# Transposing the residual on VectorE in 32x32 blocks in place of TensorE's transposes and ScalarE's copies

## The chip, the cores and the metric

The kernel runs on one core of one Trainium2 chip. The metric is the device time of one execution in microseconds (us). Three runs of the kernel before took 1252.45, 1252.47 and 1254.14 us, median 1252.47. The engines are named as in the profile: PE is TensorE's matmuls, PEld its weight loads, DVE is VectorE, ACT is ScalarE, POOL is GpSimd, SP is SyncE, which issues most transfers.

## The reference

One decoder layer over 272 tokens (16 meta tokens and 256 of the sequence), 2048 channels, all in float32:

```
h    = concat(meta, x)                                # 272 x 2048
u    = rmsnorm(h, norm_mix)
mix  = head groups of (u @ w_in)                      # 8 retention, 4 mLSTM heads
h    = h + mix @ w_out
u    = rmsnorm(h, norm_ffn)
up   = causal_dwconv(u @ w_up) + bias                 # 3 taps, 2 x 5632 channels
h    = h + (silu(gate) * val) @ w_down
out  = rmsnorm(h, norm_final)[16:]                    # the 256 tokens of the sequence
```

The residual h of the line before the last, 256 tokens by 2048 channels, is what this document follows: the kernel holds it channel-major and needs it token-major for the last addition.

## The kernel before, in words

Activations are kept channel-major: a tile has 128 channels on the partitions and the tokens along the free dimension, and 16 such slices make up the 2048 channels. `hT` (128 x 16 x 272) is the residual in this form. Every weight is split into two parts that TensorE multiplies: `load_w` (L123) brings 512 KB into `wraw` (4 buffers), ScalarE copies it to `whi` (L129, 5 buffers), and VectorE subtracts to get `wlo` (L131, 5 buffers). A "weight tile" below is one such piece. `mmk` (L134) spends 24 matmuls on a weight tile of 8 slices: 16 with `whi` (L138 and L139, on the high and the low part of the activations), then 8 with `wlo` (L141).

The stages are: input projections and attention heads, output projection, then the FFN in two halves of 22 channel blocks each. The output projection adds its result to `hT` slice by slice (`out_tile`, L508) and makes from it the scaled `uh` (ScalarE, L509) and `ul` (VectorE, L510), and the squares, which GpSimd sums into `ssq` (L517). `norm2` (L533) turns `ssq` into the normalisation row `rstd2`: a matmul (L535), ScalarE's L164 to L167, VectorE's L168, L169 and L537.

In the FFN, channel block j has two projections (gate, s = 0, and value, s = 1) of two weight tiles each. A projection is accumulated in one PSUM tile `mmps`, of which there are 4. VectorE empties it (`cu`, L559) by a multiplication with `rstd2`; the convolution, the gate and the split into `mh` and `ml` follow on ScalarE and VectorE. After the 22 blocks of a half, `mh` and `ml` are multiplied with `w_down` into 4 column blocks of 512 in token-major form, and `done` (L620) adds each to `hn`.

`hn` (128 tokens x 2 x 2048) is the residual token-major. `transposed_h` (L548) fills it, called once, at j = 1 of the first half: 32 TensorE transposes of 128x128 blocks of `hT` against `ident`, four of them into one PSUM tile `atps`, and 8 copies by ScalarE (L555). `hn` is first read by `done`, at the end of the first half.

The program is not run in the order in which it is written. The Tile framework sorts the instructions by its own timeline estimate into one fixed order for each engine when the kernel is built, so an instruction without dependences can land far ahead of its place in the code. Each engine then executes its own list strictly in that order, and an instruction that waits holds up all behind it.

Of the kernel before, what the change touches and what calls it, by code (L numbers as in the profile page):

```python
# [10 lines left out]
F32 = mybir.dt.float32  # L11
# [5 lines left out]
P = 128  # L17
# [5 lines left out]
T0 = NMETA - 2  # L23
# [60 lines left out]
def trunk(ctx: ExitStack, tc: tile.TileContext, io, out: bass.AP):  # L84
    nc = tc.nc

    def pool(name, bufs, **kw):
        return tc.tile_pool(name=name, bufs=bufs, **kw)
# [4 lines left out]
    at = ctx.enter_context(pool("at", 4, space=PSUM))  # L93
# [4 lines left out]
    hT = hpool.tile([P, KT, T], F32, name="hT")  # L98
# [6 lines left out]
    ident = consts.tile([P, P], F32, name="ident")  # L105
# [17 lines left out]
    def load_w(src, shape, to=None):  # L123
        nonlocal last_load
        raw = wpool.tile(shape, F32, name="wraw", bufs=4)
        last_load = nc.sync.dma_start(raw, src)
        to, n = (wpool, 5) if to in (None, wpool) else (to, None)
        hi = to.tile(shape, F32R, name="whi", bufs=n)
        nc.scalar.copy(hi, raw)  # L129
        lo = to.tile(shape, F32R, name="wlo", bufs=n)  # L130
        nc.vector.tensor_tensor(out=lo, in0=raw, in1=hi.bitcast(F32), op=ALU.subtract)  # L131
        return hi, lo
# [15 lines left out]
    def project(src, xh, xl, t0):  # L148

        ps = mm.tile([P, 512], F32, name="mmps")  # L150
        for half in range(2):
            half_tile(ps[:, : xh.shape[2] - t0], src, half, xh, xl, t0)
        return ps

    def table(name, after):

        with tc.issue_after(after.ins):
            return nc.scalar.preload_act_table_set(name)
# [38 lines left out]
    with pool("sq", 1, side="right") as sqp:  # L197
        for k0, k1 in [(0, 1), (1, 2)] + [(k, k + 2) for k in range(2, KT, 2)]:
# [16 lines left out]
            for k in range(k0, k1):  # L215
                i = k - k0
# [30 lines left out]
    a = _COLS["retn"][0]  # L247
    nc.vector.tensor_scalar(out=norms[:, :RH], in0=par[:, a : a + RH], scalar1=-0.5, scalar2=None, op0=ALU.mult)

    a = _COLS["mln"][0]  # L250
# [245 lines left out]
    hn = hnp.tile([P, 2, DM], F32, name="hn")  # L496
# [36 lines left out]
    def norm2():  # L533
        ms2 = at.tile([P, 512], F32, name="atps")
        nc.tensor.matmul(ms2[:, :NQ], inv_dm, ssq, start=True, stop=True)  # L535
        r = rsqrt_m2(wk2, ms2[:, :NQ], NQ, squared)
        nc.vector.tensor_scalar(out=rstd2, in0=r[:, :NQ], scalar1=-0.5, scalar2=None, op0=ALU.mult)  # L537
# [7 lines left out]
    ss4 = midp.tile([P, 2, 4], F32, name="ss4")  # L545
    junk = midp.tile([P, 512], F32, name="junk")

    def transposed_h():  # L548
        for tt in range(2):
            for q in range(4):  # L550
                ps = at.tile([P, 512], F32, name="atps")
                for j in range(4):
                    c = T0 + 2 + tt * P
                    nc.tensor.transpose(ps[:, j * P : (j + 1) * P], hT[:, 4 * q + j, c : c + P], ident)  # L554
                nc.scalar.copy(hn[:, tt, q * 512 : (q + 1) * 512], ps)  # L555

    def conv3(ps, f, name):
        u = wk2.tile([P, NQ], F32, name="cu")
        nc.vector.tensor_tensor(out=u, in0=ps[:, :NQ], in1=rstd2, op=ALU.mult)  # L559
        o = wk2.tile([P, SEQ], F32, name=name)  # L560
        nc.scalar.activation(o, u[:, 2:], AF.Identity, scale=pcol("fw", 3 * f + 2), bias=pcol("fb", f))
        for j in range(2):
            nc.vector.scalar_tensor_tensor(out=o, in0=u[:, j : j + SEQ], scalar=pcol("fw", 3 * f + j), in1=o, op0=ALU.mult, op1=ALU.add)
        return o
# [6 lines left out]
    def finish(tt):  # L571
        v, r, t = ss[:, tt : tt + 1], r0[:, tt : tt + 1], rt[:, tt : tt + 1]
        nc.vector.reduce_sum(v, ss4[:, tt, :], axis=mybir.AxisListType.X)
        nc.scalar.activation(r, v, AF.Ln, scale=1.0 / DM, bias=epsc)
        nc.scalar.activation(r, r, AF.Exp, scale=-0.5)
        nc.vector.tensor_scalar(out=v, in0=v, scalar1=-0.5 / DM, scalar2=-0.5 * EPS, op0=ALU.mult, op1=ALU.add)
        nc.vector.scalar_tensor_tensor(out=t, in0=v, scalar=r, in1=r, op0=ALU.mult, op1=ALU.mult)
        nc.vector.scalar_tensor_tensor(out=t, in0=t, scalar=1.5, in1=r, op0=ALU.add, op1=ALU.mult)
        for q in range(4):
            h = hn[:, tt, q * 512 : (q + 1) * 512]  # L580
            if q % 2 == 0:
                nc.vector.tensor_scalar(out=h, in0=h, scalar1=t, scalar2=None, op0=ALU.mult)
            else:
                nc.scalar.activation(h, h, AF.Copy, scale=t)
            nc.sync.dma_start(out[tt * P : (tt + 1) * P, q * 512 : (q + 1) * 512], h)

    NQD = NHF // 2
    for half in range(2):
        mh = midp.tile([P, NHF, SEQ], F32R, name="mh")
        ml = midp.tile([P, NHF, SEQ], F32R, name="ml")  # L590
        for jj in range(NHF):
            j = half * NHF + jj
            pair = []
            for s in range(2):
                pair.append(project(io["wu"][2 * j + s], uh, ul, 0))
                if j == 0 and s == 0:
                    norm2()
            gt = conv3(pair[0], j, "gt")
            vt = conv3(pair[1], NF + j, "vt")
            nc.scalar.activation(gt, gt, AF.Silu)  # L600
            nc.vector.tensor_tensor(out=gt, in0=gt, in1=vt, op=ALU.mult)
            copied = nc.scalar.copy(mh[:, jj, :], gt)
            nc.vector.tensor_tensor(out=ml[:, jj, :], in0=gt, in1=mh[:, jj, :].bitcast(F32), op=ALU.subtract)
            if j == 1:
                transposed_h()
        if half == 1:
            table("natural_log_exp_and_others", copied)

        def product(ps, tt, q, w):
            hi, lo = w  # L610
            rows = slice(tt * P, (tt + 1) * P)
            for i in range(2):
                k = 2 * q + i
                nc.tensor.matmul(ps, mh[:, k, rows], hi[:, i, :], start=k == 0, stop=False)  # L614
                nc.tensor.matmul(ps, ml[:, k, rows], hi[:, i, :], start=False, stop=False)  # L615
            for i in range(2):
                k = 2 * q + i
                nc.tensor.matmul(ps, mh[:, k, rows], lo[:, i, :], start=False, stop=k == NHF - 1)  # L618

        def done(ps, tt, b):  # L620
            h = hn[:, tt, b * 512 : (b + 1) * 512]
            nc.vector.tensor_tensor(out=h, in0=ps, in1=h, op=ALU.add)
            if half == 1:
                nc.scalar.activation(junk, h, AF.Square, accum_out=ss4[:, tt, b : b + 1])
                nc.gpsimd.tensor_tensor(out=h, in0=h, in1=gfin[:, b * 512 : (b + 1) * 512], op=ALU.mult)

        if half == 1:
            wk2_cm.__exit__(None, None, None)
            up_cm.__exit__(None, None, None)
            more_cm = pool("more", 4, side="right")  # L630
            more = more_cm.__enter__()
        for b in range(4):
            pss = [at.tile([P, 512], F32, name="atps") for _ in range(2)]
            last = half == 1 and b == 3

            lag = 4 if last else 0
            ws = {}
            for q in range(NQD + lag):
                if q < NQD:
                    ws[q] = load_w(io["wd"][b, half * NQD + q], [P, 2, 512], more if last and q % 2 else wpool)  # L640
                    product(pss[0], 0, q, ws[q])
                    if q == NQD - 1:
                        done(pss[0], 0, b)
                        if last:
                            finish(0)
                if q >= lag:
                    product(pss[1], 1, q - lag, ws.pop(q - lag))
            done(pss[1], 1, b)
# [84 lines left out]
```

## Time and profile before

| | us |
|---|---|
| median of three runs | 1252.47 |
| profiled execution | 1253.9 |
| its span, first to last instruction | 1252.1 |
| PE busy | 1237.2 (99%) |
| PEld busy | 1178.8 (94%) |
| DVE busy | 810.9 (65%) |
| ACT busy | 657.8 (53%) |
| mean granted TensorE clock | 0.997 |

The profiled execution is 1.4 us above the median, and 1.8 us of its time lie outside the span. The span was taken on the same program as the three runs. The busy shares are means over all stages. Times in the trace are counted from the start of the span; the output projection's last weight tile ends at 484.0 us, and the FFN begins there.

### The profile page before, as it was taken

Reading aid. Unit: us, or ns where it says so; the run is one execution under the profiler, and the core shown is the slowest. Engines: PE = TensorE matmul, PEld = TensorE weight load, DVE = VectorE, ACT = ScalarE, POOL = GpSimd, SP = SyncE. Lnnn points to the kernel's source line nnn. Section 1 sums busy time; section 2 is a strip of 40 time slices with the busy share of each in tenths; the row PEclk is TensorE's granted clock in tenths of the full one; section 3 lists DMA queues with packets and bytes.
Section 4 is the critical chain, followed back from the end, with each engine's and each line's share of the span. In section 5 each row is a group of like instructions: output and inputs, shape, how many; then the busy total and the mean of one; then the engine's idle time right before and its main releaser. Section 6 shows DMA issues by size and latency. Waiting matters only on the chain.

```text
span 1252.1 us, 22222 instructions
## 1 busy us (share of the span) xinstructions
PE 1237.2 (99%) x9094; PEld 1178.8 (94%) x9094; DVE 810.9 (65%) x1188; ACT 657.8 (53%) x885; POOL 64.1 (5%) x68
## 2 busy tenths in 40 slices
PE   8999999999999999999999999999999999999996
PEld 7999999999999999999999998888999999998885
DVE  7857677766666767667677664445776767664452
ACT  8646655655556546655555553334555555554441
POOL 0100001111110111000000000000000000000010
PEclk9999999999999999999999999999999999999999
DMA  8754554555554667555555656665655555666661
GB/s 269 228 183 136 159 156 154 174 170 173 159 166 155 178 185 218 156 185 183 185 186 179 185 177 189 192 188 185 185 183 184 175 185 184 186 181 185 189 202 68
DMA packets 63591, 224.11 MB, mean 179 GB/s; under 512 B 7388, under 2 KB 8284, under 8 KB 63360
## 3 DMA queue, kind: packets, MB, share of 16 engines
q1 hardware_dynamic: 62832, 219.92, 56.4%
q0 software_dynamic: 656, 2.76, 0.8%
q8 instruction: 71, 1.16, 0.4%
q14 instruction: 32, 0.26, 0.1%
HBM read 220.56 MB, written 2.10 MB: 178 GB/s over the span
## 4 chain that ended last, share of the span: by engine, by line
PE 98%; DVE 1%; DMA 0%; ACT 0%; issue 0%; SPq 0%; ACTq 0%; DVEq 0%
PE mmps L138 25%; PE mmps L141 25%; PE mmps L139 25%; PE atps L615 7%; PE atps L618 7%; PE atps L614 7%; PE atps L330 1%; DMA wraw<-in_w 0%; PE atps L322 0%; PE atps L307 0%; PE atps L332 0%; PE atps L331 0%; PE atps L554 0%; PE atps L323 0%; DVE xl L207 0%
## 5 line engine op out<-in xcount | busy, mean ns | idle before, releaser
L129 ACT CAST whi<-wraw 128x1024 fp32r<-128x1024 f32 x404 | 423.4, 1049 | 489.2 <-PE mmps L139 256.1
L131 DVE TENSOR_TENSOR wlo<-wraw,whi 128x1024 fp32r<-128x1024 f32 x404 | 494.9, 1226 | 200.8 <-ACT whi L129 193.6
L139 PE MATMUL mmps<-ul,whi 128*128 128x258 f32 x1408 | 345.8, 283 | 0.0
L138 PE MATMUL mmps<-uh,whi 128*128 128x258 f32 x1408 | 345.8, 282 | 0.0
L138 PEld LDWEIGHTS mmps<-uh,whi 128*128 128x128 f32 x1408 | 266.1, 189 | 0.1
L139 PEld LDWEIGHTS mmps<-ul,whi 128*128 128x128 f32 x1408 | 265.2, 188 | 0.1
L138 PE MATMUL mmps<-xh,whi 128*128 128x272 f32 (+2 forms) x880 | 224.5, 289 | 0.0
L139 PE MATMUL mmps<-xl,whi 128*128 128x272 f32 (+2 forms) x880 | 222.1, 285 | 0.0
L141 PE MATMUL mmps<-uh,wlo 128*128 128x258 f32 x1408 | 199.2, 284 | 0.0
L141 PEld LDWEIGHTS mmps<-uh,wlo 128*128 128x128 f32 x1408 | 182.4, 189 | 0.0
L138 PEld LDWEIGHTS mmps<-xh,whi 128*128 128x128 f32 x880 | 165.7, 188 | 1.3
L139 PEld LDWEIGHTS mmps<-xl,whi 128*128 128x128 f32 x880 | 165.9, 189 | 0.1
L615 PE MATMUL atps<-whi,ml 128*128 128x512 f32 x352 | 140.0, 398 | 0.0
L614 PE MATMUL atps<-whi,mh 128*128 128x512 f32 x352 | 138.0, 392 | 0.0
L141 PE MATMUL mmps<-xh,wlo 128*128 128x272 f32 (+2 forms) x880 | 129.1, 285 | 0.0
L141 PEld LDWEIGHTS mmps<-xh,wlo 128*128 128x128 f32 x880 | 116.9, 188 | 0.0
L559 DVE TENSOR_TENSOR cu<-mmps,rstd 128x258 f32<-128x258 f32 x88 | 37.6, 427 | 116.0 <-PE mmps L141 115.9
L618 PE MATMUL atps<-wlo,mh 128*128 128x512 f32 x352 | 110.4, 395 | 0.0
L615 PEld LDWEIGHTS atps<-whi,ml 128*128 128x128 f32 x352 | 66.1, 188 | 17.0
L618 PEld LDWEIGHTS atps<-wlo,mh 128*128 128x128 f32 x352 | 66.1, 188 | 16.0
L614 PEld LDWEIGHTS atps<-whi,mh 128*128 128x128 f32 x352 | 66.1, 188 | 14.9
L139 PE MATMUL mmps<-mixl,whi 128*128 128x258 f32 x256 | 63.3, 283 | 0.0
(203 smaller groups left out, 1021.5 us busy)
## 6 DMA issues: line engine op xcount, KB each, us to landing
wraw<-in_wu SPq DMA_DIRECT2D x176, 512.0 KB, 3.5
wraw<-in_wi SPq DMA_DIRECT2D x108, 512.0 KB, 3.6
wraw<-in_wd SPq DMA_DIRECT2D x88, 512.0 KB, 3.5
wraw<-in_wo SPq DMA_DIRECT2D x32, 512.0 KB, 3.6
wraw<-in_w SPq DMA_DIRECT2D x7, 320.0 KB, 5.8
out<-hn SPq DMA_DIRECT2D x8, 256.0 KB, 3.0
hT<-in_xT SPq DMA_DIRECT2D x7, 272.0 KB, 6.4
e<-in_decay POOLq DMA_DIRECT2D x8, 209.0 KB, 3.4
```

What stands on the lines that cost most here:

```text
L129: nc.scalar.copy(hi, raw)
L131: nc.vector.tensor_tensor(out=lo, in0=raw, in1=hi.bitcast(F32), op=ALU.subtract)
L138: nc.tensor.matmul(ps, hi[:, k, :], xh(kk), start=kk == first, stop=False)
L139: nc.tensor.matmul(ps, hi[:, k, :], xl(kk), start=False, stop=False)
L141: nc.tensor.matmul(ps, lo[:, k, :], xh(kk), start=False, stop=kk == last)
L330: nc.tensor.matmul(ps[:, 0:NQ], lhs(0, P), pT[:, 0:CA], start=True, stop=False)
L559: nc.vector.tensor_tensor(out=u, in0=ps[:, :NQ], in1=rstd2, op=ALU.mult)
L614: nc.tensor.matmul(ps, mh[:, k, rows], hi[:, i, :], start=k == 0, stop=False)
L615: nc.tensor.matmul(ps, ml[:, k, rows], hi[:, i, :], start=False, stop=False)
L618: nc.tensor.matmul(ps, mh[:, k, rows], lo[:, i, :], start=False, stop=k == NHF - 1)
```

## The change

`transposed_h` no longer uses TensorE, PSUM or ScalarE. It takes an index i from 0 to 3, the block of 32 channels within each slice of 128. For each of the 4 blocks a of 32 tokens and each of the 2 token tiles t, one VectorE instruction takes 32 partitions by 16 slices by 32 tokens of `hT` and writes the sixteen 32x32 blocks, each transposed, to 32 partitions of `hn`. That is 8 instructions for one i and 32 in all, each with 512 elements per partition on 32 partitions. In the code the calls are spread over j = 1 to 4.

```diff
-    def transposed_h():
-        for tt in range(2):
-            for q in range(4):
-                ps = at.tile([P, 512], F32, name="atps")
-                for j in range(4):
-                    c = T0 + 2 + tt * P
-                    nc.tensor.transpose(ps[:, j * P : (j + 1) * P], hT[:, 4 * q + j, c : c + P], ident)
-                nc.scalar.copy(hn[:, tt, q * 512 : (q + 1) * 512], ps)
+    def transposed_h(i):
+
+        src = hT[32 * i : 32 * (i + 1), :, T0 + 2 :].rearrange("p k (t a e) -> p k t a e", t=2, e=32)
+        for a in range(P // 32):
+            dst = hn[32 * a : 32 * (a + 1), :, :].rearrange("p t (k f) -> p k t f", f=P)
+            for t in range(2):
+                nc.vector.transpose(dst[:, :, t, 32 * i : 32 * (i + 1)], src[:, :, t, a, :])
...
-            if j == 1:
-                transposed_h()
+            if 1 <= j <= 4:
+                transposed_h(j - 1)
```

The built programs show where the instructions land. On VectorE, at the change from the output projection to the FFN, the list before reads as follows; the first row is the addition to the last slice of `hT`, `ul` is the last low part of the activations, L168 to L537 make `rstd2`, and L559 empties the first FFN projection:

```order
L508 TENSOR_TENSOR hT<-mmps,hT 128x258
L131 TENSOR_TENSOR wlo<-wraw,whi 128x1024
L510 SCALAR_TENSOR_TENSOR ul<-hT,par,uh 128x258
L131 TENSOR_TENSOR wlo<-wraw,whi 128x1024 x2
L168 SCALAR_TENSOR_TENSOR rt<-atps,rt 128x258
L169 SCALAR_TENSOR_TENSOR r_5863<-rt,r_5863 128x258
L537 TENSOR_SCALAR rstd_84<-r_5863 128x258
L559 TENSOR_TENSOR cu<-mmps,rstd_84 128x258
```

Between the last `hT` and the first `cu` stand 3 weight tiles' `wlo` (one row of one and one row of two) and four small operations. The list of the changed kernel has at the same place, first part:

```order
L508 TENSOR_TENSOR hT<-mmps,hT 128x258
L131 TENSOR_TENSOR wlo<-wraw,whi 128x1024
L554 STREAM_TRANSPOSE hn<-hT 32x16x32 x9
L510 SCALAR_TENSOR_TENSOR ul<-hT,par,uh 128x258
L554 STREAM_TRANSPOSE hn<-hT 32x16x32 x6
L131 TENSOR_TENSOR wlo<-wraw,whi 128x1024
L554 STREAM_TRANSPOSE hn<-hT 32x16x32 x3
L168 SCALAR_TENSOR_TENSOR rt<-atps,rt 128x258
L554 STREAM_TRANSPOSE hn<-hT 32x16x32 x2
L131 TENSOR_TENSOR wlo<-wraw,whi 128x1024
L554 STREAM_TRANSPOSE hn<-hT 32x16x32 x4
```

All calls have moved ahead of the place where they stand in the code: 24 of the 32 transposes stand in these rows, behind the last `hT` and among the steps that make `rstd2`. The rest follows on VectorE, with the tiles' own numbers (`wlo_6246` is the low part of the thirteenth weight tile of the FFN; `cu_5933` empties the first projection, `mmps_5800`):

```order
L131 TENSOR_TENSOR wlo_6045<-wraw_6041,whi_6043 128x1024 [waits DMAHW4_49,PE_49,Activation_49]
L131 TENSOR_TENSOR wlo_6100<-wraw_6096,whi_6098 128x1024 [waits DMAHW5_49,PE_49,Activation_49]
L554 STREAM_TRANSPOSE hn_4707<-hT_70 32x16x32 x4
L169 SCALAR_TENSOR_TENSOR r0_5863<-rt_5867,r0_5863 128x258 [waits DVE_49]
L554 STREAM_TRANSPOSE hn_4707<-hT_70 32x16x32
L131 TENSOR_TENSOR wlo_6130<-wraw_6126,whi_6128 128x1024 [waits DMAHW6_49,PE_49,Activation_49]
L554 STREAM_TRANSPOSE hn_4707<-hT_70 32x16x32 x3
L131 TENSOR_TENSOR wlo_6161<-wraw_6157,whi_6159 128x1024 [waits DMAHW7_49,PE_49,Activation_49]
L131 TENSOR_TENSOR wlo_6191<-wraw_6187,whi_6189 128x1024 [waits DMAHW0_49,PE_49,Activation_49]
L537 TENSOR_SCALAR rstd2_84<-r0_5863 128x258 [waits DVE_49]
L131 TENSOR_TENSOR wlo_6246<-wraw_6242,whi_6244 128x1024 [waits DMAHW1_49,PE_49,Activation_49]
L558 TENSOR_TENSOR cu_5933<-mmps_5800,rstd2_84 128x258 [waits DVE_49]
```

The first `cu` now stands behind all 32 transposes and behind eight `wlo` that follow the first transpose (one and one in the fence above, and six here). On TensorE the 32 transposes are gone, and at the start of the fifth projection, `mmps_6095`, which is the next user of the PSUM buffer of `mmps_5800`, the list reads:

```order
L141 MATMUL mmps_6010<-uh_4711,wlo_6045 128x258 [waits DVE_49]
L141 MATMUL mmps_6010<-uh_4711,wlo_6045 128x258 x7
L138 MATMUL mmps_6095<-uh_4711,whi_6098 128x258 [waits DVE_49,Activation_49]
L139 MATMUL mmps_6095<-ul_4712,whi_6098 128x258
```

Before, 16 of the transposes stood between the two projections here; now the fifth projection follows directly, with a wait for VectorE.

## The prediction

> **What bounds the kernel now.** I read the page's busy table and the chain that ended last first.
>
> ```profile
> span 1252.1 us, 22222 instructions
> PE 1237.2 (99%) x9094; PEld 1178.8 (94%) x9094; DVE 810.9 (65%) x1188; ACT 657.8 (53%) x885; POOL 64.1 (5%) x68
> PE 98%; DVE 1%; DMA 0%; ACT 0%; issue 0%; SPq 0%; ACTq 0%; DVEq 0%
> L131 DVE TENSOR_TENSOR wlo<-wraw,whi 128x1024 fp32r<-128x1024 f32 x404 | 494.9, 1226 | 200.8 <-ACT whi L129 193.6
> ```
>
> TensorE is the bound: it is busy nearly throughout and carries 98% of the chain. So a matmul removed is time saved, and a microsecond in which TensorE stands still is a microsecond lost, since nothing later has slack to give it back. VectorE's 65% is a mean; what matters is how far it may fall behind at the place of the change. Next came the transposes themselves and the timeline around them.
>
> ```profile
> L554 PE MATMUL atps<-ident,hT x32: 270/273/273, 507.6 to 513.3; 128*128 128x128 f32 x32
> 507.61 1.91 PE L554 MATMUL atps<-ident,hT 128*128 128x128 f32 x16
> 509.27 0.37 PE L138 MATMUL mmps<-uh,whi 128*128 128x258 f32 x1
> 502.03 0.43 DVE L559 TENSOR_TENSOR cu<-mmps,rstd 128x258 f32<-128x258 f32 x1 [0.50 <-PE mmps L141]
> 507.81 0.43 DVE L559 TENSOR_TENSOR cu<-mmps,rstd 128x258 f32<-128x258 f32 x1 [1.55 <-PE mmps L141]
> 517.09 0.43 DVE L559 TENSOR_TENSOR cu<-mmps,rstd 128x258 f32<-128x258 f32 x1 [1.61 <-PE mmps L141]
> 522.87 0.43 DVE L559 TENSOR_TENSOR cu<-mmps,rstd 128x258 f32<-128x258 f32 x1 [1.51 <-PE mmps L141]
> ```
>
> A `cu` starts when TensorE has finished a projection. These follow one another by 5.78 us (502.03 to 507.81, and 517.09 to 522.87); across the transposes it is 9.28 us.
>
> **What is removed.** 9.28 − 5.78 = 3.5 us of TensorE; the first 16 transposes, 507.61 to 509.27, give 1.66, which doubled is 3.3. I take **−3.5 us**, and it is on the bounding engine. ScalarE's eight copies go too, worth nothing: ScalarE waits for buffers that TensorE frees (its 53%).
>
> **What is added: 32 VectorE instructions of unknown price.** The trace has no transpose on VectorE. Each has 512 elements per partition. The rows nearest to it:
>
> ```profile
> L213 DVE TENSOR_TENSOR wlo<-wraw,whi 128x512 fp32r<-128x512 f32 x7 | 4.8, 686 | 1.1 <-ACT whi L211 1.1
> L559 DVE TENSOR_TENSOR cu<-mmps,rstd 128x258 f32<-128x258 f32 x88 | 37.6, 427 | 116.0 <-PE mmps L141 115.9
> L582 DVE TENSOR_SCALAR hn<-hn,frt 128x512 f32<-128x512 f32 x4 | 1.8, 484 | 0.1
> L537 DVE TENSOR_SCALAR rstd<-r 128x258 f32<-128x258 f32 x1 | 0.3, 297 | 0.0
> L262 DVE TENSOR_TENSOR kT<-kT,rstd 4x272 f32<-4x272 f32 x1 | 0.4, 430 | 0.0
> 493.55 1.22 DVE L131 TENSOR_TENSOR wlo<-wraw,whi 128x1024 fp32r<-128x1024 f32 x1
> 494.68 1.00 DVE L563 SCALAR_TENSOR_TENSOR gt<-cu,par,gt 128x256 f32<-128x256 f32 x2
> ```
>
> L559 to L131 (427 ns for 258, 1226 ns for 1024 elements) is 1.04 ns per element and 158 ns fixed. L262 shows that 4 partitions cost what 128 do, so using 32 partitions at a time saves nothing: the transposes cost four times what whole-width ones would. At one element per step each takes 0.69 us (the 512-element row, 686 ns). Independent neighbours can overlap by 0.08 us or so (493.55 + 1.22 − 494.68 = 0.09), so the low side of this case is 0.61; one block's 32 further steps for filling would give 0.72. Single-source operations in SBUF run about twice as fast (L537, 297 ns); for 512 elements that is 158 + 267 = 0.43, less overlap 0.35, the **lower bound**. Two steps per element, as a 1024-element operation, give 1.23 us, the **upper bound**. I take 0.69: a transpose moves single elements between partitions, and that row has its size.
>
> The Trainium skill, "VectorE: DVE Perf Modes", section "The three transpose paths", gives 311 ns for a 128x128 bf16 transpose on VectorE, in 32x32 blocks only; at its 0.96 GHz a further 384 elements make 0.71 us, an estimate, by which the sum below would be 0.7 us higher. Its rules for kernel authors give a 128x128 transpose to TensorE if PSUM will do, which speaks against the change. No run here shows either yet.
>
> **Where they lie.** All 32 have been sorted ahead of the first `cu`, into the start of the FFN, where VectorE must also deliver `wlo` and `rstd2`. I replay VectorE's list from rows:
>
> ```profile
> 484.03 0.28 PE L138 MATMUL mmps<-uh,whi 128*128 128x258 f32 x1
> 484.57 1.22 DVE L131 TENSOR_TENSOR wlo<-wraw,whi 128x1024 fp32r<-128x1024 f32 x1
> 485.70 0.98 DVE L510 SCALAR_TENSOR_TENSOR ul<-hT,par,uh 128x258 fp32r<-128x258 f32 x1
> 485.67 0.74 POOL L517 TENSOR_TENSOR ssq<-ssq,s2b 128x258 f32<-128x258 f32 x1 [0.63 <-ACT s2b L516]
> 491.95 0.43 DVE L168 SCALAR_TENSOR_TENSOR rt<-atps,rt 128x258 f32<-128x258 f32 x1 [0.56 <-ACT rt L167]
> 492.41 0.43 DVE L169 SCALAR_TENSOR_TENSOR r<-rt,r 128x258 f32<-128x258 f32 x1
> 493.20 0.43 DVE L559 TENSOR_TENSOR cu<-mmps,rstd 128x258 f32<-128x258 f32 x1
> 506.88 1.05 ACT L129 CAST whi<-wraw 128x1024 fp32r<-128x1024 f32 x1 [1.57 <-issue]
> wraw<-in_wu SPq DMA_DIRECT2D x176, 512.0 KB, 3.5
> ```
>
> The first transpose starts at 484.57 + 1.22 = 485.8, when the last `hT` is written. From there to the end of the first `cu` VectorE has: 32 transposes of d us; eight `wlo`, 9.6 (1.2 each: 1.22, starting up to 0.09 early); L168, L169, L537 and `cu`, 0.43 + 0.43 + 0.30 + 0.43 = 1.6; and the last `ul`, 0.5. (L510 takes 0.98 here beside GpSimd's addition, 485.67, and half that elsewhere; the first transposes will now meet this addition in its place, which evens out.) The sum is 11.7 + 32 d, so `cu` ends at **497.5 + 32 d**: at 0.69, 519.6.
>
> TensorE meanwhile: the first eight FFN weight tiles (numbered from 0) run from 484.03 to 507.61, where the transposes started before. They fill all four `mmps`, and the fifth projection needs the buffer that the first `cu` frees. What else they need comes in time or just late. The last `ul` would come at 485.8 + 9 d + 0.5 = 492.5, but was moved behind in TensorE's list too, to some 494.5 by its pace of 2.89 us a tile (half of 5.78). The `wlo` of tiles 5, 6 and 7 come at about 497.8, 502.9 and 506.9; TensorE asks for them at about 500.7, 503.6 and 506.6. So TensorE is held for 0.3 us there and then stands until `cu`: together 519.6 − 507.6 = **12.0 us**, against none before. VectorE, in turn, waits for nothing in this stretch: the `wraw` behind a `wlo` comes some 3.5 us after its buffer is free, and `whi` another 1.05 later (506.88).
>
> Afterwards, `whi` and `wlo` of tiles 8 to 12 are ready when TensorE resumes, 14 us of work; the two delayed channel blocks' gates and convolutions, some 8 us on VectorE and ScalarE by the same rows, are done before tile 13's `wlo` is asked for. So no second gap follows, and none of the first is recovered.
>
> **The clock.** A pause of TensorE costs more than itself, as the start of this trace shows:
>
> ```profile
> 19.69 0.28 PE L139 MATMUL mmps<-xl,whi 128*128 128x262 f32 x1
> 21.22 0.39 PE L141 MATMUL atps<-xh,wlo 128*128 128x272 f32 x1 [1.25 <-DVE wlo L213]
> 21.60 0.43 PE L138 MATMUL atps<-xh,whi 128*128 128x272 f32 x1
> 24.95 0.28 PE L141 MATMUL mmps<-xh,wlo 128*128 128x262 f32 x1
> 25.07 0.29 PE L138 MATMUL atps<-xh,whi 128*128 128x272 f32 x1
> 23.00:24.00 1.00, 1.00 (x6) 1.00 (x6) 1.00 (x1) 0.99 (x2) 0.00 (x0) 0.50 0.97 377
> ```
>
> After a gap of 1.25 us in an already sparse stretch the granted clock was 0.50, and from 21.60 to 24.95 the 15 matmuls came 0.22 us apart in place of 0.12: 15 × 0.10 = **1.5 us** more. A gap of 12 us should bring the same once; a price of nothing is the other bound.
>
> The Trainium skill, "TensorE: Matmul & The Clock Gate", section "HAM oscillation — how this bites in real kernels", puts the drop at gaps over about 3.4 us; by that rule too a 12 us gap pays it, and this trace shows the drop after less.
>
> **The sum.** −3.5 + 12.0 + 1.5 = **+10.0 us**. On the profiled execution (span 1252.1, in all 1253.9) that is a span of 1262.1 and 1263.9 in all; the median of the runs lies 1.4 below the profiled one, so I forecast 1252.5 + 10.0 = **1262.5 us**. With d from 0.61 to 0.73 and the clock price from 0 to 1.5, this case runs from +5.9 (9.4 − 3.5) to +11.3: 1258 to 1264. Break-even is a gap of 2.0 us (2.0 + 1.5 = 3.5), `cu` at 509.6, so d = 0.38.
>
> **Rivals.**
>
> *Transposes at twice the rate* (0.35 us). For it: they have one source, in SBUF, as L537 has. Against: L537 does not cross partitions. `cu` would be ready at 508.7 but for its neighbour in the list, `wlo` of tile 12, whose `whi` waits for TensorE to finish tile 7's L139; 506.88 + 1.05, then 1.22 and 0.43 put `cu` at 509.7. The gap is 2.1, the sum −1.4 to +0.1: about 1251.5, **not slower**. At 0.43 `cu` ends at 511.3: +0.2 to +1.7.
>
> *The gap doesn't arise.* If VectorE's list caught up by its idle third, only −3.5 would be left: **1249.0**. The page's 65% speaks for it; the fixed list against it, since the first `cu` cannot pass the transposes.
>
> *Half the rate* (1.23 us). `cu` ends at 536.9, the gap is 29.3, the sum +27.3: **1279.8**. For it: 32-bit elements, rows of only 32, and a filling of the block that may not overlap the emptying. Against: no row with two steps per element except special operations.
>
> **How the numbers follow.** My case 0.70, twice the rate 0.10, no gap 0.05, slower transposes 0.15. A difference under 0.2% (2.5 us) can't be told from none here. Slower comes from my case and the slow one, 0.85; the fast one is mostly no difference, 0.10; faster needs the gap away, 0.05. The likeliest case alone has 1258 to 1264. The range takes in the fast rates, and on the slow side prices up to about 1.05 us (1274): 1252 to 1274 leaves out the missing gap and most of the slow case, under 2 in 10. The two bounds of d give 1251 and 1280.
>
> **What would show it.** L554 as a VectorE group of 32 with a mean near 0.69 us; starts between 485.8 and 517; a TensorE gap of about 12 us ending when the first `cu` ends, near 519.6, on `mmps`; the granted clock at 0.50 for some 3 us behind it; no further gap; TensorE's steps across j = 1 at 5.78. The forecast is wrong if the mean is under 0.4 us or far over 0.75, if the first `cu` starts near 493 as before, or if TensorE runs on past tile 7.

## The result

| | before | changed |
|---|---|---|
| median, us | 1253.76 (5 runs, 1252.45 to 1254.46) | 1262.63 (5 runs, 1261.79 to 1262.83) |
| ratio | | 1.0076, 95% interval 1.0065 to 1.0087 |
| profiled execution, span in us | 1252.1 | 1260.9 |

The changed kernel is slower by 0.76%, 9.5 us by the interval's centre (8.9 between the two medians). Forecast were 1262.5 us and 10.0 us more than before.

Its page shows a TensorE that is idle at one place. These are the span, the 40 slices of TensorE's busy share and of its clock, and two groups of part 5 (busy us, mean ns of one, then the idle time ahead of them and what ended it):

```profile
span 1260.9 us, 22186 instructions
PE   8999999999999999699999999999999999999996
PEclk9999999999999999799999999999999999999999
L138 PE MATMUL mmps<-uh,whi 128*128 128x258 f32 x1408 | 346.6, 283 | 11.2 <-DVE cu L558 11.2
L131 DVE TENSOR_TENSOR wlo<-wraw,whi 128x1024 fp32r<-128x1024 f32 x404 | 494.7, 1226 | 197.4 <-ACT whi L129 192.7
```

In the seventeenth slice, which begins at 504 us, TensorE falls to 6 tenths and its clock to 7. L138 waited 11.2 us for a `cu`; before, the same group waited for nothing:

```profile
L138 PE MATMUL mmps<-uh,whi 128*128 128x258 f32 x1408 | 345.8, 282 | 0.0
```

(Line numbers behind the edit are smaller by one in the changed kernel: `cu` is L558.) The price of a transpose, in the group by shape, is

```profile
L554 DVE STREAM_TRANSPOSE hn<-hT 32x512 f32<-32x512 f32 x32 | 21.1, 685 | 0.4
```

685 ns each, 21.1 us in all. VectorE's timeline from the last `hT` to the first `cu` (start, duration, then the operation and how many in a row) is the replay of the prediction with its real numbers:

```profile
482.91 0.43 DVE L508 TENSOR_TENSOR hT<-mmps,hT 128x258 f32<-128x258 f32 x1 [0.44 <-PE mmps L141]
483.26 1.22 DVE L131 TENSOR_TENSOR wlo<-wraw,whi 128x1024 fp32r<-128x1024 f32 x1
484.39 5.93 DVE L554 STREAM_TRANSPOSE hn<-hT 32x512 f32<-32x512 f32 x9
490.35 0.49 DVE L510 SCALAR_TENSOR_TENSOR ul<-hT,par,uh 128x258 fp32r<-128x258 f32 x1
490.87 4.04 DVE L554 STREAM_TRANSPOSE hn<-hT 32x512 f32<-32x512 f32 x6
494.93 1.22 DVE L131 TENSOR_TENSOR wlo<-wraw,whi 128x1024 fp32r<-128x1024 f32 x1
...
511.39 2.02 DVE L554 STREAM_TRANSPOSE hn<-hT 32x512 f32<-32x512 f32 x3
513.45 2.36 DVE L131 TENSOR_TENSOR wlo<-wraw,whi 128x1024 fp32r<-128x1024 f32 x2
515.73 0.29 DVE L537 TENSOR_SCALAR rstd<-r 128x258 f32<-128x258 f32 x1
515.93 1.22 DVE L131 TENSOR_TENSOR wlo<-wraw,whi 128x1024 fp32r<-128x1024 f32 x1
517.06 0.75 DVE L558 TENSOR_TENSOR cu<-mmps,rstd 128x258 f32<-128x258 f32 x2
```

No row of this stretch carries a wait: VectorE works without a pause from 483.26 to 517.81, and what it does last is what TensorE needs first. On TensorE the same place reads:

```profile
500.53 0.28 PE L138 MATMUL mmps<-uh,whi 128*128 128x258 f32 x1
505.33 1.13 PE L141 MATMUL mmps<-uh,wlo 128*128 128x258 f32 x8
517.63 0.55 PE L138 MATMUL mmps<-uh,whi 128*128 128x258 f32 x1 [11.16 <-DVE cu L558]
521.21 1.69 PE L141 MATMUL mmps<-uh,wlo 128*128 128x258 f32 x8
524.67 1.13 PE L141 MATMUL mmps<-uh,wlo 128*128 128x258 f32 x8
```

The eighth weight tile ends at 506.46, the ninth starts at 517.63, when the first `cu` has given a PSUM buffer back. Then the clock: from the resumption to the L141 of the tenth tile 524.67 − 517.63 = 7.04 us pass; in step, from 500.53 to 505.33 over as many matmuls, 4.80. So 2.2 us are lost behind the gap. These rows of 1 us each show the granted clock (the third number from the end) falling in the gap and coming back some 5 us after the end of it:

```profile
508.00:509.00 1.00, 0.00 (x0) 0.00 (x0) 0.97 (x3) 0.26 (x1) 0.00 (x0) 0.92 0.90 229
509.00:510.00 1.00, 0.00 (x0) 0.00 (x0) 0.97 (x2) 0.79 (x1) 0.00 (x0) 0.50 0.67 266
521.00:522.00 1.00, 1.00 (x6) 1.00 (x6) 0.99 (x3) 1.00 (x3) 0.00 (x0) 0.50 0.01 4
522.00:523.00 1.00, 1.00 (x9) 1.00 (x8) 1.00 (x4) 0.95 (x2) 0.00 (x0) 0.76 0.00 0
523.00:524.00 1.00, 1.00 (x11) 1.00 (x10) 1.00 (x2) 0.00 (x0) 0.00 (x0) 1.00 0.00 0
```

The sum is −3.5 + 11.2 + 2.2 = +9.9. The spans differ by 8.8 only, since the profiled executions already differ where the programs are the same: the last `hT` is at 484.22 in the one of before, which ran at half clock from 21.51 to 24.92 us, and at 482.91 here, 1.3 us earlier, and the profile of the changed kernel shows no half clock at that place. From that instruction to the end it is 1252.1 − 484.22 = 767.9 before and 1260.9 − 482.91 = 778.0 after: **+10.1 us**, which the sum explains but for 0.2. The experiments are compared in the same way below, as "from the last hT".

### The profile page after: what moved, and what is told of

It reads as the page before. It is cut to its first block, busy times and chain, and to the rows that moved or that the text cites. A ratio compares the mean times of both kernels' runs of the same rounds, so it can differ in the third digit from the quotient of the medians.

```text
span 1260.9 us, 22186 instructions
## 1 busy us (share of the span) xinstructions
PE 1235.5 (98%) x9062; PEld 1177.2 (93%) x9062; DVE 829.7 (66%) x1220; ACT 653.0 (52%) x877; POOL 62.1 (5%) x68
## 4 chain that ended last, share of the span: by engine, by line
PE 95%; DVE 3%; issue 1%; ACT 0%; DMA 0%; SPq 0%; ACTq 0%; DVEq 0%
PE mmps L138 24%; PE mmps L141 24%; PE mmps L139 24%; PE atps L614 7%; PE atps L617 7%; PE atps L613 6%; DVE hn L554 1%; DVE wlo L131 1%; PE atps L330 1%; PE atps L322 0%; PE atps L307 0%; PE atps L332 0%; DMA hT<-in_xT 0%; PE atps L331 0%; DVE xl L207 0%
## 5 line engine op out<-in xcount | busy, mean ns | idle before, releaser
L138 PE MATMUL mmps<-uh,whi 128*128 128x258 f32 x1408 | 346.6, 283 | 11.2 <-DVE cu L558 11.2
L138 PEld LDWEIGHTS mmps<-uh,whi 128*128 128x128 f32 x1408 | 267.1, 190 | 11.4 <-issue 11.3
L138 PE MATMUL mmps<-xh,whi 128*128 128x272 f32 (+2 forms) x880 | 224.3, 289 | 0.0
L141 PE MATMUL mmps<-uh,wlo 128*128 128x258 f32 x1408 | 199.4, 284 | 0.0
L141 PEld LDWEIGHTS mmps<-uh,wlo 128*128 128x128 f32 x1408 | 183.0, 190 | 0.0
L138 PEld LDWEIGHTS mmps<-xh,whi 128*128 128x128 f32 x880 | 165.6, 188 | 1.3
L141 PE MATMUL mmps<-xh,wlo 128*128 128x272 f32 (+2 forms) x880 | 129.1, 285 | 0.0
L141 PEld LDWEIGHTS mmps<-xh,wlo 128*128 128x128 f32 x880 | 116.8, 188 | 0.0
L558 DVE TENSOR_TENSOR cu<-mmps,rstd 128x258 f32<-128x258 f32 x88 | 37.3, 426 | 111.2 <-PE mmps L141 111.2
```

Source lines behind the costliest of these rows:

```text
L138: nc.tensor.matmul(ps, hi[:, k, :], xh(kk), start=kk == first, stop=False)
L141: nc.tensor.matmul(ps, lo[:, k, :], xh(kk), start=False, stop=kk == last)
```

## The experiments

**Theory.** A transpose on VectorE is no dearer than forecast and would fit into VectorE's idle time. The loss comes from all 32 standing ahead of the first `cu`, in a list that VectorE must follow: TensorE uses up its four `mmps` and stands. **Rivals:** VectorE has no room for this work wherever it stands; the broken thing is the chain that makes `rstd2`; TensorE is held by late weights (`wlo`), not by `mmps`; TensorE's transposes were partly hidden, so that the change had nothing to gain.

### No transposition at all

```diff
-    def transposed_h():
-        for tt in range(2):
...
-                nc.scalar.copy(hn[:, tt, q * 512 : (q + 1) * 512], ps)
+    def transposed_h():
+        with tc.issue_after(squared[1].ins):
+            nc.gpsimd.memset(hn, 0.0)
```

Here `squared[1]` is GpSimd's last addition to `ssq`.

> The residual isn't transposed at all: hn is filled with zeros by GpSimd behind its last addition to ssq, so the last addition of the residual is left out. TensorE's 32 transposes and ScalarE's 8 copies are gone and nothing is put on VectorE. Theory (the removal is worth 3.5 us, the rest of the change is a gap): 3.5 us under the kernel before, about 1250.3 against 1253.8. Rival (TensorE's transposes were partly hidden, and the gap in the changed kernel is smaller than its trace says): under 1.5 us gained, above 1252.3.

Measured: 1249.3 us against 1252.54, ratio 0.9972 (0.9961 to 0.9983). From the last hT 1247.6 − 483.23 = 764.4, 3.5 under before. TensorE's 32 transposes were on the critical path with their full price, and 3.5 us is all that the change could bring.

### The calls held where the code has them

```diff
-            nc.vector.tensor_tensor(out=ml[:, jj, :], in0=gt, in1=mh[:, jj, :].bitcast(F32), op=ALU.subtract)
+            split = nc.vector.tensor_tensor(out=ml[:, jj, :], in0=gt, in1=mh[:, jj, :].bitcast(F32), op=ALU.subtract)
             if 1 <= j <= 4:
-                transposed_h(j - 1)
+                with tc.issue_after(split.ins):
+                    transposed_h(j - 1)
```

> The changed kernel with one thing undone: the eight transposes of each call are held behind the last VectorE step (ml) of their own channel block, j = 1 to 4, so that they stand where the code has them. Theory (only the pile of 32 at the start costs, for it delays the first cu): no gap, since 8 x 0.66 = 5.3 us come to a block in which VectorE idles 2.9 of 11.6 us, and the 2.4 us too many per block, 9.5 us after four, stay inside the lead that VectorE has on TensorE (4 weight tiles, 11.5 us); so the full gain of the removal, about 1250.3. Rival (VectorE has no room for 21 us of transposes in four blocks, wherever they stand): a second-half gap of 2 to 9 us with the clock's price on top, 1253 to 1262.

Measured: 1249.14 us, ratio 0.9972 (0.9961 to 0.9983); from the last hT 1248.3 − 484.00 = 764.3, 3.6 under before and the same as without any transposition. TensorE waits nowhere in the FFN. On VectorE's timeline two of the four groups of eight stand like this:

```profile
512.09 5.21 DVE L554 STREAM_TRANSPOSE hn<-hT 32x512 f32<-32x512 f32 x8
517.34 0.43 DVE L558 TENSOR_TENSOR cu<-mmps,rstd 128x258 f32<-128x258 f32 x1
517.68 2.35 DVE L131 TENSOR_TENSOR wlo<-wraw,whi 128x1024 fp32r<-128x1024 f32 x2
...
529.51 5.22 DVE L554 STREAM_TRANSPOSE hn<-hT 32x512 f32<-32x512 f32 x8
534.76 0.43 DVE L558 TENSOR_TENSOR cu<-mmps,rstd 128x258 f32<-128x258 f32 x1
535.11 2.35 DVE L131 TENSOR_TENSOR wlo<-wraw,whi 128x1024 fp32r<-128x1024 f32 x2
```

Behind each of these two a `cu` comes without a wait and two `wlo` in one go: VectorE falls behind by up to 5 us, makes it up, and TensorE never waits for it. The same 32 instructions with the same total cost 13.7 us more or less by their place alone (778.0 against 764.3).

### Two to a channel block

```diff
-            if 1 <= j <= 4:
-                transposed_h(j - 1)
+            if 1 <= j <= 16:
+                with tc.issue_after(split.ins):
+                    transposed_h((j - 1) // 4, (j - 1) % 4)
```

The two arguments are now the block i of channels and the block a of tokens.

> The same 32 transposes, two to a channel block, j = 1 to 16, held behind ml. 1.3 us come to a block with 2.9 us of idle VectorE. Theory: wholly hidden, 3.5 us under the kernel before, about 1250.3, and the same as without any transposition. Rival (transposes on VectorE cost TensorE something by themselves, through memory ports or semaphores): above 1252.

Measured: 1248.71 us, ratio 0.9972 (0.9962 to 0.9981); from the last hT 1247.5 − 483.16 = 764.3. The work of the transposes is unchanged, as the group shows:

```profile
L553 DVE STREAM_TRANSPOSE hn<-hT 32x512 f32<-32x512 f32 x32 | 20.7, 681 | 0.2
```

20.7 us of VectorE cost TensorE nothing here. This version computes all that the reference asks for and beats both kernels: 0.28% under the one of before, and by the two medians 13.9 us under the changed one (1262.63 − 1248.71; 13.7 from the last hT). It can't be told apart from the one that holds eight to a block.

### Held behind rstd2 only

```diff
-        nc.vector.tensor_scalar(out=rstd2, in0=r[:, :NQ], scalar1=-0.5, scalar2=None, op0=ALU.mult)
+        return nc.vector.tensor_scalar(out=rstd2, in0=r[:, :NQ], scalar1=-0.5, scalar2=None, op0=ALU.mult)
...
-                    norm2()
+                    normed = norm2()
...
-                transposed_h(j - 1)
+                with tc.issue_after(normed.ins):
+                    transposed_h(j - 1)
```

> The changed kernel, but all transposes are held behind the one instruction that makes rstd2, and sorted freely behind it: 5 stand ahead of the first cu, 27 between the first and the third. Theory (what counts is how much VectorE work stands ahead of the cu that frees the next mmps buffer): rstd2 comes at about 493 as in the kernel before, the first two cu come in time, but the third, which the seventh projection needs at about 519, comes at about 527: a gap of 8 us, later, and 2 us for the clock, less the 3.5: about 1261, 7 above the kernel before. Rival (the chain that makes rstd2 was what the transposes broke; whole, it costs nothing): about 1250.3, no gap.

Measured: 1259.42 us, ratio 1.0052 (1.0038 to 1.0066); from the last hT 1256.9 − 482.46 = 774.4, 6.6 above before. VectorE's list and the place on TensorE where it shows:

```profile
491.11 0.30 DVE L537 TENSOR_SCALAR rstd<-r 128x258 f32<-128x258 f32 x1
491.32 3.31 DVE L554 STREAM_TRANSPOSE hn<-hT 32x512 f32<-32x512 f32 x5
494.67 0.43 DVE L558 TENSOR_TENSOR cu<-mmps,rstd 128x258 f32<-128x258 f32 x1
...
502.94 0.43 DVE L558 TENSOR_TENSOR cu<-mmps,rstd 128x258 f32<-128x258 f32 x1
...
525.49 0.42 DVE L558 TENSOR_TENSOR cu<-mmps,rstd 128x258 f32<-128x258 f32 x1
526.05 0.55 PE L138 MATMUL mmps<-uh,whi 128*128 128x258 f32 x1 [8.50 <-DVE cu L558]
```

`rstd2` is in time, and so are the first two `cu`; the gap has moved to the third, as the theory said: 8.5 us of gap, 1.5 of clock, less 3.5, makes 6.5. The chain that makes `rstd2` is not the cause by itself. What counts is how much VectorE work stands ahead of the `cu` that TensorE needs next.

### Five mmps buffers, before and after

```diff
-    mm = ctx.enter_context(pool("mm", 4, space=PSUM))
-    at = ctx.enter_context(pool("at", 4, space=PSUM))
+    mm = ctx.enter_context(pool("mm", 5, space=PSUM))
+    at = ctx.enter_context(pool("at", 3, space=PSUM))
```

The control, the kernel before with this edit:

> The kernel before with five mmps buffers in place of four and three atps in place of four. The control for the next run. Theory: TensorE never waits for mmps before the change, so no gain from a fifth; three atps may hold up the heads: 1253.8, or up to 3 us more.

Measured: 1253.98 us, ratio 1.0011 (1.0001 to 1.0020); from the last hT 1252.2 − 484.34 = 767.9, the same as with four. A fifth buffer by itself brings nothing.

The changed kernel with it:

> The changed kernel with the same buffers: five mmps, three atps. Theory (in the changed kernel TensorE stands because the first cu hasn't freed an mmps, while the weights lie ready): TensorE goes on for one projection more, 5.8 us, and the first cu has one wlo more ahead of it, 1.2 us; so the gap falls from 11.2 to about 6.5 us, and the time is about 5 us above the control, not 9. Rival (TensorE would have stood for the late wlo as well): the gap stays at 9 to 11 us and the difference to the control at about 9 us.

Measured: 1259.48 us, ratio to the kernel before 1.0052 (1.0037 to 1.0067), so 5.5 us over the control by the medians; from the last hT 1257.2 − 484.61 = 772.6, 4.7 over the control's.

```profile
513.11 1.23 PE L141 MATMUL mmps<-uh,wlo 128*128 128x258 f32 x8 [0.16 <-DVE wlo L131]
520.46 0.55 PE L138 MATMUL mmps<-uh,whi 128*128 128x258 f32 x1 [6.11 <-DVE cu L558]
```

The gap is 6.1 us in place of 11.2. TensorE did go on for one projection when it had a buffer for it, and then stood again for `cu`; late `wlo` held it for 0.2 us only. So the held resource is `mmps`. With one more buffer TensorE stops 6.2 us later, counted from the last hT (a projection's 5.8 us and 0.4 of small delays), and `cu` comes 1.1 later, since one more `wlo` stands ahead of it: 11.2 − 6.2 + 1.1 = 6.1.

### Every transpose twice

```diff
-                nc.vector.transpose(dst[:, :, t, 32 * i : 32 * (i + 1)], src[:, :, t, a, :])
+                for _ in range(2):
+                    nc.vector.transpose(dst[:, :, t, 32 * i : 32 * (i + 1)], src[:, :, t, a, :])
```

> The changed kernel with every transpose issued twice, 64 in all (the second repeats the first's work). 50 of them stand ahead of the first cu, with the same eight wlo. Theory: 18 x 0.66 = 11.9 us more before the first cu, a gap of 23 us, and a second one of about 2 us at the seventh projection, since 14 more stand behind the first two cu: 1275 to 1277. The clock's price of a gap is the same after 23 us as after 11 (one weight tile takes 5.1 us in place of 2.9). Rival (the price of the clock grows with the gap's length): a cold stretch of twice the length, 2 us more.

Measured: 1278.27 us, ratio 1.0200 (1.0183 to 1.0217); from the last hT 1276.5 − 483.95 = 792.6, 24.7 above before. 

```profile
531.48 0.55 PE L138 MATMUL mmps<-uh,whi 128*128 128x258 f32 x1 [23.73 <-DVE cu L559]
546.97 0.36 PE L138 MATMUL mmps<-uh,whi 128*128 128x258 f32 x1 [1.37 <-DVE cu L559]
```

The 18 transposes more ahead of the first `cu` lengthen the gap by 23.7 − 11.2 = 12.5 us, 0.70 each; the second gap is 1.4. The sum −3.5 + 23.7 + 1.4 + 2.4 (clock, read as above: 538.70 − 531.48 − 4.80) = 24.0 leaves 0.7 open. The measured time is 1.3 above the upper end of what was expected.

### The clock behind a gap, profiled anew

Three of the kernels were profiled again, unaltered, since the slow stretch behind the gap had cost 1.5 and 1.6 us behind the two shorter gaps and 2.2 and 2.4 behind the longer ones.

> The changed kernel unaltered, profiled anew, for the price of the clock behind one and the same gap. The first profile lost 2.2 us in the slow stretch behind an 11.2 us gap; gaps of 6.1 and 8.5 us lost 1.5, one of 23.7 us lost 2.4. If the length of the gap sets the price, the loss here is 2.2 again, within 0.1. If it depends on when TensorE resumes, it is another value between 1.5 and about 3.

> The same once more: 2.2 us if the length of the gap sets the price of the clock, another value if the moment at which TensorE resumes does.

> The changed kernel with five mmps and three atps, profiled anew: 1.5 us lost behind its 6.1 us gap if the length of the gap sets the price of the clock; a value that differs from run to run, up to about 3, if the moment of resuming does.

> Every transpose issued twice, profiled anew: 2.4 us lost behind its 23.7 us gap if the length of the gap sets the price of the clock; possibly as little as 1.5 if the moment of resuming does.

Measured were 1262.38, 1262.63, 1259.48 and 1277.43 us, one run each. In the table the loss is counted from the resumption to the second L141 behind it, less 4.80; the time at half clock and the moment of its end are read from the granted clock. In the first profile of the changed kernel, for example, it fell at 508.84 (0.92 in the row from 508 above is 0.84 us at full and 0.16 at half) and was back at 522.48 (0.76 in the row from 522):

| kernel | gap, us | at half clock in all, us | from resuming to full clock, us | lost behind the gap, us |
|---|---|---|---|---|
| changed, three profiles | 11.16, 11.16, 11.17 | 13.65, 13.65, 13.65 | 4.9, 4.4, 5.7 | 2.2, 2.1, 2.6 |
| five mmps, two profiles | 6.11, 6.12 | 6.83, 6.83 | 3.3, 3.5 | 1.6, 1.6 |
| held behind rstd2 | 8.50 | 6.83 | 3.1 | 1.5 |
| every transpose twice, two profiles | 23.73, 23.72 | 27.31, 27.31 | 5.3, 5.4 | 2.4, 2.5 |

The two further profiles of the changed kernel, at the same place:

```profile
517.61 0.55 PE L138 MATMUL mmps<-uh,whi 128*128 128x258 f32 x1 [11.16 <-DVE cu L558]
524.46 1.13 PE L141 MATMUL mmps<-uh,wlo 128*128 128x258 f32 x8
```
```profile
517.26 0.55 PE L138 MATMUL mmps<-uh,whi 128*128 128x258 f32 x1 [11.17 <-DVE cu L558]
524.67 1.13 PE L141 MATMUL mmps<-uh,wlo 128*128 128x258 f32 x8
```

6.85 and 7.41 us in place of 7.04: one and the same gap cost 2.1, 2.2 and 2.6 us, so its length does not set the price alone. The granted clock shows what does. The times at half clock are 4, 2 and 8 times 3.41 us, and the one at the start of the kernel before (21.51 to 24.92) is 3.41 once. In all thirteen profiles, whole multiples of 3.41 us also separate one change of the clock from the next, from the first full clock to the end of the FFN, and the point at which the counting starts differs from one execution to the next. So time falls into stretches of 3.41 us, and the clock changes only where one ends. It fell only behind a stretch in which TensorE had 1.9 us of work or less, and behind every one with under 1.8; a stretch with 2.04 us (held behind `rstd2`) did not bring it down. It came back behind the first stretch with 3.1 us of work or more; one with 2.3 us (the third profile of the changed kernel) did not bring it back. The loss is a little under half of the time from resuming to the return: a TensorE that resumes near the start of a stretch loses some 1.5 us, and one that resumes in the middle is slow for the rest of that stretch as well. By this the gap's length counts only through where its two ends fall.

The Trainium skill, "TensorE: Matmul & The Clock Gate", section "What's actually happening", gives a window of about 3.4 us that runs freely, so that the point of change depends on where in it the matmuls begin; these profiles agree, with 3.41 us.

## Why the prediction was right

*What is removed, −3.5 us.* Right: without any transposition the time from the last hT falls by 3.5.

*The price, 0.69 us of a possible 0.35 to 1.23.* Right: 0.685 us, 0.66 from one to the next (9 in 5.93), which is the size of the row of 512 elements on 128 partitions (686 ns) that the price was taken from. Twice and half the rate are both refuted. The estimate from the Trainium skill's figure ("VectorE: DVE Perf Modes", "The three transpose paths"), 0.71, is 0.03 above the measured mean.

*The replay of VectorE's list.* Right in mechanism, 0.8 us too long: 12.0 us of gap were forecast and 11.2 measured. Counted from the last `hT`, the first `cu` was to end 519.6 − 484.2 = 35.4 us later; its row starts 34.15 us later (517.06 − 482.91), and one `cu` takes 0.43, so the first ended 34.6 later. Of the 0.8 us, 0.6 are the transposes: with what follows each group they fill 21.5 us of the list in place of 32 × 0.69 = 22.1. The 0.3 us for late `wlo`, which the 12.0 already held, did not come as a wait: TensorE's waits in the FFN are that one of 11.2 us.

*The clock, 1.5 us.* Mis-sized: 2.2 in the first profile, above the 0 to 1.5 that the likeliest case allowed for. The price was taken from the slow stretch at the kernel's start, 3.35 us long, in which TensorE had work throughout; here TensorE resumed in the middle of a stretch of 3.41 us, which did not bring the clock back, and the next one had to pass as well, 4.9 us together. This error and the one of the gap have opposite signs and 0.7 and 0.8 us of size, so it is luck that the sum, +10.0 against +10.1, is better than its terms.

*No later gap, and nothing recovered.* Right: the one wait for `cu` is the only one in the FFN.

*The rivals.* That VectorE's list would catch up by its idle third fell for the reason given, and the runs with held calls show both sides of it: the idle third is real and holds all 32 transposes, but only if the list is in an order that lets it.

*The base.* The forecast started from a median of 1252.47. Beside the experiments the unaltered kernel had medians of 1252.54 and a single run of 1252.52, beside the changed one a median of 1253.76. Over that last one 1262.5 is 8.7 us more, not 10.0, so it is luck that it lies 0.1 from the measured 1262.63; what bears out the forecast of the change is the +10.1 from the last hT. The runs of the unaltered kernel lie at two levels, 1251.9 to 1252.9 and 1253.5 to 1254.5. The profiles suggest a reason, which is not shown, since the single runs have no trace: where half clock falls between 20 and 25 us of the start (before, eight to a block, the first profile with every transpose twice) the last hT is at 483.95 to 484.22; in the other profiles with four `mmps`, where it falls earlier or not at all, at 482.46 to 483.23.

## What to carry to other kernels

Work moved off the bounding engine onto a half-idle one is free only where the receiving engine's list gives it room, so read the order in which the built program issues it, not the place where the code calls it. Sum the work that stands ahead of the next thing that the bounding engine needs (here the `cu` that frees a PSUM buffer) and compare it with the lead that the buffers give. Where a scheduler may hoist work that is wanted only much later, tie it behind an instruction of its own stage: here that alone turned 0.76% lost into 0.28% won. And count a pause of the bounding engine at more than its length: here 1.5 to 2.6 us more, by the moment at which it resumes.

## What was not expected of the hardware

The slow clock behind one and the same 11.2 us gap cost 2.1, 2.2 and 2.6 us in three profiles, more than the 1.5 us that the kernel's start had shown, since it comes back only at the end of a stretch of 3.41 us that was nearly full of work.

The first transposes ran beside GpSimd's last addition to `ssq`:

```profile
484.35 0.74 POOL L517 TENSOR_TENSOR ssq<-ssq,s2b 128x258 f32<-128x258 f32 x1 [0.62 <-ACT s2b L516]
```

`ul` (L510) had taken 0.98 us beside that addition before and takes 0.49 here, out of its way, so the prediction's text let the transposes bear the difference, though its sum of 11.7 + 32 d does not add it. They did not bear it: the nine that began with it took 5.93 us, 0.66 each, as the later groups did. Why the one slows down and the other doesn't is open.
